# Attention with a bias on one core: q and k of twelve head pairs transposed by DMA instead of by TensorE

## The chip, the core and the metric

The kernel runs on one core of one Trainium2 chip. The metric is device microseconds of one execution; a kernel is given by the median of its runs. The engines are PE (TensorE; PEld is its weight load, which runs beside the matmuls), DVE (VectorE), ACT (ScalarE), POOL (GpSimd) and SP (SyncE, which here only issues DMAs). DMAs issued from SP and ACT go through hardware queues, those issued from POOL through a software queue; all of them run on the core's 16 DMA engines.

## The reference

q, k and v are [4, 8, 1024, 64] in float32, the bias is [1, 1, 1024, 1024] and the same for all 32 heads.

```python
scores = scale * np.matmul(q, k.transpose(0, 1, 3, 2))      # scale = 1/8
scores = scores + bias
scores_max = np.max(scores, axis=-1, keepdims=True)
attn = np.exp(scores - scores_max) / (np.sum(np.exp(scores - scores_max), axis=-1, keepdims=True) + 1e-8)
return np.matmul(attn, v).astype(np.float32)
```

## The kernel before

**Tiling.** The 32 heads are 16 pairs. Rows of the sequence are numbered (p c): partition p holds rows 8p to 8p+7, and chunk c, one of NCH = 8, is the 128 rows with that c. The unit of work is a slot (x, c, h, start): chunk c of the queries of head h, against all 1024 keys, with the scores (keys on the partitions, 8 blocks of 128 queries, 1024 float32 for each partition) in PSUM place x of three. There are 256 slots.

**Scores by difference.** The bias of a chunk is multiplied into a place only where `start` is set (192 matmuls at L220 in all). For the next head in the same place the kernel adds its scores and takes off those of the head before in one matmul of 128 contraction rows: 64 rows hold k and q of the new head, the other 64 hold k and the negated q of the old one. So four arrays [128, 8, 128] stand for each pair:

- `ko`, `qo`: rows 0 to 63 the even head (q negated), rows 64 to 127 the odd head of the same pair. They serve the odd head.
- `ke`, `qe`: rows 0 to 63 the even head of the pair, rows 64 to 127 the odd head of the pair before (q negated). They serve the even head.
- `qs`, `qz`: q of an even head over rows of zeros, for slots with `start`.

**From the inputs to these arrays.** POOL loads k and q of a pair with a cast to bf16 (`load_k` L133, `load_q` L141) into `land` tiles, of which there are three of each kind. DVE lays the two heads side by side (`side_by_side` L148, tiles `kr` and `qr`, two of each). PE transposes 8 blocks of 128x128 into a PSUM bank (`transposes` L177). DVE copies the bank to SBUF (`copy_out`: `ko` L184, `qo` with signs L186), and then fills the second homes of k and q (`double`: `ke` L195, `qe`, `qs` and `qz` L197): rows 0 to 63 of the same pair's `ke`, rows 64 to 127 of the next pair's. Some of the q doubles go to POOL. The ring of arrays has nine places (RING). V goes by two DMAs of 128 KB for each pair (`load_v` L158) straight into `vall`, whose 65th column is 1; only pairs 0 to 3 have V in a landing tile that DVE copies (L472).

**The work of a slot.** PE fills the place with 8 matmuls (`fill_half` L223). ACT takes the exponential of 1024 columns (`exp` L237) into one of nine `E` tiles in bf16; no maximum is taken off. PE multiplies the 8 blocks of E with V and the column of ones (`av` L296) into a PSUM bank of up to seven slots. DVE empties the bank (`evac`: reciprocal of the sums L304, product into `ob` L308, of which there are two; `od` L312 for blocks that DVE exponentiated), and SP stores the result (L313, L321). For 16 slots the exponential runs on DVE, in seven steps (`d_steps` L257 to L280: `dy`, `df`, `dpw`, `dy`, `db`, `db`, `de`).

**The order.** The pairs go in groups of 4, 6 and 6 (GROUPS). Within a group all heads pass once with three chunks (rounds of three slots), then with chunks 3 and 4, then with the three others. So a new pair of the group is first wanted every six slots, and then no new one until the next group. Pairs 4 to 9 are the second group, 10 to 15 the third. `may_d` names the slots that may go to DVE.

The order on every engine is written out by a planner inside the kernel: a loop at the end keeps a clock for PE, ACT and DVE, and at each step lets the engine go on that can start first. It works with fixed costs (an exponential 906 ns, a fill 450, a bank multiplication 265), with due times `ready[...]`, `raw_at`, `land_at`, `v_at` of arrays, layouts and loads, and with priorities for DVE. `pieces` is the list of transpositions that PE still has to make, in the order of the pairs; a piece may go when its pair is at most AHEAD = 60 slots away and a ring place is free. A pair's loads are issued once the q layout three pairs before it is written. What the planner writes is a fixed program; at run time the engines only wait for semaphores.

Of the kernel before, what the change touches and what calls it, by code (L numbers as in the profile page):

```python
# [16 lines left out]
def kernel(  # L17
# [35 lines left out]
    raw = ctx.enter_context(tc.tile_pool(name="raw", bufs=2))  # L53
    kq = ctx.enter_context(tc.tile_pool(name="kq", bufs=RING))
# [19 lines left out]
    b0f = consts.tile([P, S], F32)  # L74
    q0f = consts.tile([P, 2, C0, D], F32)
    q0r = consts.tile([P, 2, NCH - C0, D], BF)
    k0f = consts.tile([P, 2, NCH, D], F32)
# [49 lines left out]
    may_d = [x[0] == 2 and 24 < s < NS - 12 and not any(y[3] for y in slots[s:s + 4]) for s, x in enumerate(slots)]  # L127

    raws, lands, arrs = {}, {}, {}
# [5 lines left out]
    def load_q(pr, cs):  # L135
        if pr == 0:
            lands[0, 0] = q0r
        elif (pr, 0) not in lands:
            lands[pr, 0] = land.tile([P, 2, NCH, D], BF, name="q16")
        to = lands[pr, 0] if pr == 0 else lands[pr, 0][:, :, cs, :]  # L140
        nc.gpsimd.dma_start(out=to.rearrange("p t c d -> p t (c d)"),  # L141
                            in_=qf[pr][:, :, cs.start * D:cs.stop * D])

# [15 lines left out]

    def arrays(pr):  # L160
        if pr not in arrs:
            t = {x: kq.tile([P, NCH, P], BF, name=x) for x in (("ko", "ke", "qo", "qe") if pr else ("ko", "qo"))}
            if pr in split_pair:
                t["qs"] = qs
            if pr in first_pair:
                t["qz"] = qz[group_of[pr] % 2]
            arrs[pr] = t
        return arrs[pr]

    def linked(pr):  # L170
        return pr + 1 < NP
# [28 lines left out]
    def parts(pr, which):  # L200
        return ([0] if pr else []) + ([1] if linked(pr) else []) + (
            [] if which else [2] * (pr in split_pair) + [3] * (pr in first_pair))
# [96 lines left out]
    def evac(b):  # L299
        po, units = bank[b]  # L300
        n = len(units)
        own = [s for s in units if batch_of[s] == b and s not in dslots]
        rs = small.tile([P, 7, 1], F32, name="rs")
        nc.vector.reciprocal(rs[:, :n, :], po[:, :n, D:D1])  # L304
        m = len(own)
        ob = op.tile([P, 6, D], F32, name="ob")
        if m:
            nc.vector.tensor_tensor(ob[:, :m, :], po[:, :m, :D], rs[:, :m, :].to_broadcast([P, m, D]), op=ALU.mult)  # L308
        for j in range(m, n):
            x, c, h, start = slots[units[j]]  # L310
            od = op.tile([P, D], F32, name="od")
            nc.vector.tensor_tensor(od[:], po[:, j, :D], rs[:, j, :].to_broadcast([P, D]), op=ALU.mult)  # L312
            nc.sync.dma_start(out=of[:, h, c, :], in_=od[:])  # L313

        j = 0
        while j < m:
            x, c, h, start = slots[own[j]]
            i = j + 1
            while i < m and slots[own[i]][1:3] == (c + i - j, h):
                i += 1  # L320
            nc.sync.dma_start(out=of[:, h, c:c + i - j, :], in_=ob[:, j:i, :])  # L321
            j = i

    with tc.manual_schedule():
# [66 lines left out]
        EXP = 906  # L391
        T0 = 7400.0
# [14 lines left out]
        q_items += [(p, 0, 0, NCH) for p in range(GROUPS[0], NP)]  # L407
        k_items = [(p, 1, 0, NCH) for p in range(1, NP)]
        n1 = GROUPS[0] - 1
        pieces = [y for x in zip(k_items[:n1], q_items[:n1]) for y in x] + q_items[n1:n1 + GROUPS[0]]  # L410
        pieces += [y for x in zip(k_items[n1:], q_items[n1 + GROUPS[0]:]) for y in x]
# [12 lines left out]
        waiting, free_lands, loads = [], set(), list(range(GROUPS[0], NP))  # L424
        AHEAD = 60
# [16 lines left out]
        def arrange(pr, which, c0, n):  # L442

            if (pr, which, c0) not in land_at:
                waiting.append((pr, which, c0, n))
                return
            urgent = need_at[pr, which, c0] - next_fill < 12
            cost = 60 + 35 * n

            def run(t2):  # L450
                side_by_side(pr, which, slice(c0, c0 + n))
                raw_at[pr, which, c0] = t2 + cost + L_DVE
                if which == 0 and c0 + n == NCH:
                    free_lands.add(pr)
                    while loads and loads[0] - 3 in free_lands:
                        load(loads.pop(0), t2)
            dve_q.append((land_at[pr, which, c0], 0 if urgent else 2, cost, run))

        def load(pr, t):
            load_k(pr)  # L460
            load_q(pr, slice(0, NCH))
            land_at[pr, 1, 0] = dma(pool(t, 750), 1900)
            land_at[pr, 0, 0] = dma(pool(t, 750), 1900)
            load_v(pr)
            v_at[pr] = dma(pool(0, 1900), 5500)
            for x in [x for x in waiting if x[0] == pr]:
                waiting.remove(x)
                arrange(*x)

# [59 lines left out]
        def pe_cands():  # L529
# [59 lines left out]
            if pieces:  # L589
# [4 lines left out]
                if ((pr, which, c0) in raw_at and next_fill >= need - AHEAD and (ring < 0 or last_slot[ring] < next_fill)  # L594
# [6 lines left out]
                    if r < 1e11:  # L601
# [5 lines left out]
                        def end(t, pr=pr, which=which, c0=c0, n=n, tag=tag, cost=cost):  # L607
# [8 lines left out]
                            def run(t2):  # L616
# [3 lines left out]
                                if which:  # L620
                                    ready["ko", pr] = done + L_DVE
                                else:
# [11 lines left out]
        def close(b, tag, t):  # L634
# [4 lines left out]
            def run(t2):  # L639
                evac(b)  # L640
# [67 lines left out]
        while next_fill < NS or next_act < len(acts) or avq or dav or dve_q:  # L708
# [10 lines left out]
            if p:  # L719
                c.append((p[0], 2))  # L720
            if not c:
# [9 lines left out]
            elif who == 1:  # L731
                dve_q.remove(d)
                t_dve = t + d[2]
                d[3](t)
            else:
# [32 lines left out]
```

## Time and profile before

| what | value |
|---|---|
| runs | median 247.41 us of 3 (247.38 to 248.35) |
| profiled execution | 247.3 us, its span 245.5 us (first to last instruction), granted TensorE clock 0.992 |
| ACT, exponentials (L237) | 241 instructions, 223.6 us busy |
| PE, value matmuls (L296), score matmuls (L223) | 89.1 us (1920, with another 6.7 us for DVE's blocks); 76.5 and 62.3 us (1024 and 832, and 192 with `qz` and `qs`) |
| PE, transpositions (L177) | 256 matmuls, 22.5 us busy |
| DVE, 16 exponentials (L257 to L280) | 119.5 us |
| DMA queues | POOL's software queue 36304 packets, 14.06 MB, 50.0% of 16 engines' time; SP's 17664 packets, 9.12 MB, 13.5% |
| stores on SP | 117, median 2.1 us to landing (1.4 to 7.9) |
| loads of k on POOL | 15, 3.7 to 10.3 us to landing, median 5.5 |

How it is read: the busy times of PE overlap, since matmuls are pipelined, so a busy PE is not a PE at its limit. A line stands for all instructions that a source line writes, whatever pair they belong to, so stages are told apart by stretches of the span. The DMA share is the sum of packet times over 16 engines; where several queues are served at once it goes over 1.

### The profile page before, as it was taken

Reading aid. Unit: us, or ns where it says so; the run is one execution under the profiler, and the core shown is the slowest. Engines: PE = TensorE matmul, PEld = TensorE weight load, DVE = VectorE, ACT = ScalarE, POOL = GpSimd, SP = SyncE. Lnnn points to the kernel's source line nnn. Section 1 sums busy time; section 2 is a strip of 40 time slices with the busy share of each in tenths; the row PEclk is TensorE's granted clock in tenths of the full one; section 3 lists DMA queues with packets and bytes.
Section 4 is the critical chain, followed back from the end, with each engine's and each line's share of the span. In section 5 each row is a group of like instructions: output and inputs, shape, how many; then the busy total and the mean of one; then the engine's idle time right before and its main releaser. Section 6 shows DMA issues by size and latency. Waiting matters only on the chain.

```text
span 245.5 us, 10300 instructions
## 1 busy us (share of the span) xinstructions
PE 223.2 (91%) x4554; PEld 211.3 (86%) x4554; DVE 214.5 (87%) x370; ACT 226.7 (92%) x245; POOL 61.9 (25%) x82
## 2 busy tenths in 40 slices
PE   7879999999989898999999988898999999999981
PEld 2779899999989897989999988788999998998871
DVE  3669963989999999999999999999999999499991
ACT  3689999999999989999999998999999999999991
POOL 8837566041313504325000374000000000000000
PEclk9999999999999999999999999999999999999996
DMA  6999999999998697998741391110121021020211
GB/s 211 203 202 171 215 199 198 196 134 110 148 104 109 76 145 127 140 92 133 92 83 31 73 120 29 40 47 19 40 61 42 27 63 28 19 69 27 67 40 37
DMA packets 54155, 24.34 MB, mean 99 GB/s; under 512 B 32352, under 2 KB 53088, under 8 KB 54112
## 3 DMA queue, kind: packets, MB, share of 16 engines
q0 software_dynamic: 36304, 14.06, 50.0%
q1 hardware_dynamic: 17664, 9.12, 13.5%
q8 instruction: 35, 0.57, 1.0%
q10 hardware_dynamic: 144, 0.52, 0.6%
q14 instruction: 8, 0.07, 0.1%
HBM read 29.36 MB, written 8.39 MB: 154 GB/s over the span
## 4 chain that ended last, share of the span: by engine, by line
DVE 41%; PE 29%; ACT 17%; issue 9%; DMA 2%; ACTq 0%; SPq 0%; DVEq 0%
PE pl L223 17%; ACT E L237 17%; PE po L296 7%; DVE qo L186 4%; DVE dy L257 4%; DVE ke L195 4%; DVE ob L308 4%; DVE qe L197 3%; DVE de L280 3%; DVE ko L184 3%; PE pl L220 3%; DVE db L276 3%; DVE dy L269 3%; DVE db L269 2%; DMA k0f<-in_k_dram 2%
## 5 line engine op out<-in xcount | busy, mean ns | idle before, releaser
L237 ACT ACTIVATE E<-pl 128x1024 bf16<-128x1024 f32 (+1 forms) x241 | 223.6, 1072 | 9.1 <-PE pl L223 8.1
L296 PE MATMUL po<-vall,E 128*128 128x65 bf16 x1920 | 89.1, 194 | 6.1 <-DVE ob L308 2.2
L296 PEld LDWEIGHTS <-E 128*128 128x128 bf16 x1920 | 76.5, 98 | 7.9 <-DVE ob L308 3.0
L223 PE MATMUL pl<-qo,ko 128*128 128x128 bf16 x1024 | 76.5, 219 | 3.3 <-ACT E L237 1.6
L223 PEld LDWEIGHTS <-ko 128*128 128x128 bf16 x1216 | 72.4, 98 | 6.6 <-issue 4.6
L223 PE MATMUL pl<-qe,ke 128*128 128x128 bf16 x832 | 62.3, 219 | 4.0 <-DVE qe L197 1.8
L223 PEld LDWEIGHTS <-ke 128*128 128x128 bf16 x832 | 49.7, 98 | 6.2 <-issue 4.5
L308 DVE TENSOR_TENSOR ob<-po,rs 128x384 f32<-128x384 f32 (+3 forms) x44 | 22.9, 521 | 1.8 <-DVE rs L304 0.3
L257 DVE TENSOR_SCALAR dy<-pl 128x1024 int32<-128x1024 f32 x16 | 19.5, 1220 | 4.7 <-ACT E L237 3.5
L133 POOL DMA_DIRECT2D k<-in_k_dram x15 | 11.1, 740 | 46.1 <-DVE kr L148 31.8
L158 POOL DMA_DIRECT2D vall<-in_v_dram x24 | 21.1, 882 | 0.9 <-issue 0.6
L141 POOL DMA_DIRECT2D q<-in_q_dram x18 | 12.9, 719 | 33.2 <-DVE qr L148 26.6
L269 DVE SCALAR_TENSOR_TENSOR dy<-df 128x1024 f32<-128x1024 f32 x16 | 19.5, 1218 | 0.2
L276 DVE SCALAR_TENSOR_TENSOR db<-db,dpw 128x1024 f32<-128x1024 f32 x16 | 19.5, 1219 | 0.2
L280 DVE SCALAR_TENSOR_TENSOR de<-dy,db 128x1024 bf16<-128x1024 f32 x16 | 19.5, 1219 | 0.2
L269 DVE SCALAR_TENSOR_TENSOR db<-df 128x1024 f32<-128x1024 f32 x16 | 19.5, 1219 | 0.0
L220 PE MATMUL pl<-ident,braw 128*128 128x128 bf16 x192 | 16.0, 226 | 0.1
L195 DVE COPY ke<-ko 64x1024 bf16<-64x1024 bf16 x30 | 14.5, 484 | 0.8
L184 DVE COPY ko<-px 128x1024 bf16<-128x1024 bf16 (+1 forms) x17 | 11.1, 651 | 4.2 <-PE px L177 4.2
L186 DVE TENSOR_SCALAR qo<-px,sgn 128x1024 bf16<-128x1024 bf16 (+2 forms) x20 | 12.7, 637 | 2.2 <-PE px L177 2.0
L197 DVE TENSOR_SCALAR qe<-qo 64x1024 bf16<-64x1024 bf16 (+2 forms) x33 | 13.4, 407 | 0.9
L304 DVE RECIPROCAL rs<-po 128x5 f32<-128x5 f32 (+4 forms) x44 | 8.4, 192 | 6.5 <-PE po L296 6.2
(50 smaller groups left out, 153.8 us busy)
## 6 DMA issues: line engine op xcount, KB each, us to landing
out_dram<-ob SPq DMA_DIRECT2D x53, 96.0 KB, 1.9
k<-in_k_dram POOLq DMA_DIRECT2D x15, 256.0 KB, 5.5
q<-in_q_dram POOLq DMA_DIRECT2D x12, 256.0 KB, 5.5
vall<-in_v_dram POOLq DMA_DIRECT2D x24, 128.0 KB, 6.1
out_dram<-ob SPq DMA_DIRECT2D x33, 64.0 KB, 3.3
braw<-in_bias_dram POOLq DMA_DIRECT2D x7, 256.0 KB, 7.3
v<-in_v_dram POOLq DMA_DIRECT2D x4, 256.0 KB, 6.4
b0f<-in_bias_dram ACTq DMA_DIRECT2D x1, 512.0 KB, 4.5
```

The costliest lines, as they stand in the source:

```text
L158: nc.gpsimd.dma_start(out=vall[:, 2 * pr + t, :, :D], in_=vf[pr, :, t])
L186: nc.vector.tensor_scalar(t["qo"][:, cs, :], px[:], sgn[:], None, op0=ALU.mult)
L195: w.tensor_copy(to["ke"][rows, cs, :], t["ko"][rows, cs, :])
L220: nc.tensor.matmul(to, braw[:, c, :].rearrange("p (kp kc) -> p kc kp", kc=NCH)[:, kc, :], ident8[:], start=i == 0, stop=False, skip_group_ ...
L223: nc.tensor.matmul(to, kk[:, kc, :], qq[:, c, :], start=False, stop=True, skip_group_check=True)
L237: nc.scalar.activation(e[:, i:i + n].rearrange("p b x -> p (b x)"), places[slots[s][0]][:, i:i + n].rearrange("p b x -> p (b x)"), ACTF.Ex ...
L257: w.tensor_scalar(y[:], places[slots[s][0]].rearrange("p b x -> p (b x)"), scale * LOG2E * 65536.0, 127.0 * 65536.0, op0=ALU.mult, op1=ALU ...
L269: w.scalar_tensor_tensor(o[:], t["f"][:], c, t["f"][:], op0=ALU.add, op1=ALU.mult)
L276: w.scalar_tensor_tensor(t["b"][:], t["b"][:], V2, t["p"].bitcast(BF), op0=ALU.add, op1=ALU.mult)
L280: w.scalar_tensor_tensor(etile[s].rearrange("p c q -> p (c q)"), t["a"], V1, t["b"][:], op0=ALU.add, op1=ALU.mult)
L296: nc.tensor.matmul(po[:, j, :], etile[s][:, kc, :], vall[:, h, kc, :], start=j == 0 and kc == 0, stop=kc == NCH - 1, skip_group_check=True)
L308: nc.vector.tensor_tensor(ob[:, :m, :], po[:, :m, :D], rs[:, :m, :].to_broadcast([P, m, D]), op=ALU.mult)
```

## The change

For pairs 4 to 15, TensorE's transpositions, the PSUM bank that they pass through, the copies out of it and the doublings of k and q are replaced as follows. Pairs 0 to 3 stay as they were.

- DVE lays out three bf16 tiles for each pair in place of two (`layout_steps`): `kr` as before (one copy of 1024 elements for each partition, L186); `qr` with the even head negated, in two half steps (L190, L195); and `q2`, three buffers, which holds this pair's even head beside the negated odd head of the pair before. Its first half is written with the pair itself (L196), its second with the pair before (`removed`, L150).
- SP issues a DMA transposition of each of them, SBUF to SBUF, straight into the array that PE reads: `kr` to `ko`, `qr` to `qo`, `q2` to `qe` (`turn`, L200), 36 in all, each of 256 KB.
- SP issues plain DMAs for k's second home, rows 0 to 63 of `ke` from the same pair's `ko` (L552) and rows 64 to 127 from the pair before (L541, L555), and for `qs` and `qz` where a pair starts a group or a chunk of slots (L572): 28 in all, each of 64 rows of 2 KB.
- All SP issues, the stores among them, pass through one planned queue (`sp_q`). `evac` hands back its stores, with the `od` ones behind the `ob` ones.
- A pair's V is loaded when the next pair's k and q are (pair 15's with its own).
- The landing buffers of the first bias chunk and of the first k (`b0f`, `k0f`) move into the pool of DVE's exponential (tiles `df` and `db`).
- `may_d` ends 18 slots before the end instead of 12. In the program that comes out, 17 slots have their exponential on DVE, and PE has 64 transposing matmuls.

The diff, cut to its core:

```diff
+    raw2 = ctx.enter_context(tc.tile_pool(name="raw2", bufs=3))
...
-    b0f = consts.tile([P, S], F32)
+    b0f = dp.tile([P, S], F32, name="df")
...
-    k0f = consts.tile([P, 2, NCH, D], F32)
+    k0f = dp.tile([P, S], F32, name="db").rearrange("p (t c d) -> p t c d", t=2, d=D)
...
-    may_d = [x[0] == 2 and 24 < s < NS - 12 and not any(y[3] for y in slots[s:s + 4]) for s, x in enumerate(slots)]
+    may_d = [x[0] == 2 and 24 < s < NS - 18 and not any(y[3] for y in slots[s:s + 4]) for s, x in enumerate(slots)]
...
+    def removed(pr, cs):
+        if pr + 1 not in q2:
+            q2[pr + 1] = raw2.tile([P, NCH, 2, D], BF, name="q2")
+        nc.vector.tensor_scalar(q2[pr + 1][:, cs, 1, :], lands[pr, 0][:, 1, cs, :], -1.0, None, op0=ALU.mult)
...
+    def layout_steps(pr, which):
+        l = lands[pr, which]
+        if which:
+            raws[pr, 1, 0] = t = raw.tile([P, NCH, 2, D], BF, name="kr")
+            return [(340, lambda: nc.vector.tensor_copy(t.rearrange("p c t d -> p t c d"), l[:]))]
+        def first():
+            raws[pr, 0, 0] = t = raw.tile([P, NCH, 2, D], BF, name="qr")
+            nc.vector.tensor_scalar(t[:, :, 0, :], l[:, 0], -1.0, None, op0=ALU.mult)
+        def last():
+            removed(pr, slice(0, NCH))
+        steps = [first, lambda: nc.vector.tensor_copy(raws[pr, 0, 0][:, :, 1, :], l[:, 1]),
+                 lambda: nc.vector.tensor_copy(q2[pr][:, :, 0, :], l[:, 0])]
+        return [(HALF, f) for f in steps + [last] * (pr + 1 < NP)]
+
+    def turn(to, of):
+        nc.sync.dma_start_transpose(to[:], of.rearrange("p c t d -> p c (t d)"))
...
+        ISSUE, TURN, COPY = 70, 4500, 3000
...
-        q_items += [(p, 0, 0, NCH) for p in range(GROUPS[0], NP)]
-        k_items = [(p, 1, 0, NCH) for p in range(1, NP)]
+        k_items = [(p, 1, 0, NCH) for p in range(1, GROUPS[0])]
...
-            load_v(pr)
-            v_at[pr] = dma(pool(0, 1900), 5500)
+            for p in [pr - 1] * (pr > GROUPS[0]) + [pr] * (pr + 1 == NP):
+                load_v(p)
+                v_at[p] = dma(pool(0, 1900), 4800)
...
+        def advance():
+            while turns:
+                pr, which = turns[0]
+                ring = pr + 1 - RING
+                if ((pr, which, 0) not in land_at or next_fill < first_slot[pr] - AHEAD
+                        or ring >= 0 and last_slot[ring] >= next_fill
+                        or pr < GROUPS[0] + 2 and any(y[1] == which for y in pieces)
+                        or pr >= GROUPS[0] + 2 and (pr - 2, which) not in turned
+                        or which == 0 and pr == GROUPS[0] and left_q2
...
+                    return
+                turns.pop(0)
+                prio = 0 if first_slot[pr] - next_fill < 12 else 2
+                steps = layout_steps(pr, which)
...
+                    dve_q.append((max(land_at[pr, which, 0], turned.get((pr - 2, which), 0)), prio, cost, run))
...
+        def turn_k(pr, t):
...
+            turn(a["ko"], raws[pr, 1, 0])
+            done = turned[pr, 1] = ready["ko", pr] = t + TURN
+            def copies(t2):
+                nc.sync.dma_start(out=a["ke"][:D], in_=a["ko"][:D])
+                ready["ke", pr] = t2 + COPY
+                if pr + 1 < NP:
+                    nc.sync.dma_start(out=arrays(pr + 1)["ke"][D:], in_=a["ko"][D:])
...
+            sp_q.append((done, copies))
+
+        def turn_q(pr, t):
...
+            turn(a["qo"], raws[pr, 0, 0])
+            turn(a["qe"], q2[pr])
+            t_sp += ISSUE
+            done = turned[pr, 0] = t + TURN + 1000
...
-                evac(b)
+                for to, of_ in evac(b):
+                    sp_q.append((t2 + cost + L_DVE, lambda t3, to=to, of_=of_: nc.sync.dma_start(out=to, in_=of_)))
```

## The prediction

> **What bounds the kernel now.** I read the page's busy shares first, then its slices, then a table of stages, then who waited for whom in two of them.
>
> The page, parts 1 and 2 (busy us, share of the span, instructions; then tenths in 40 slices of 6.1 us):
> ```profile
> PE 223.2 (91%) x4554; PEld 211.3 (86%) x4554; DVE 214.5 (87%) x370; ACT 226.7 (92%) x245; POOL 61.9 (25%) x82
> ...
> ACT  3689999999999989999999998999999999999991
> ...
> DMA  6999999999998697998741391110121021020211
> ```
> Three engines stand near 90%, so the average decides nothing. ACT runs 240 of the 256 score blocks' exponentials, one after the other, from 9.4 us to 240.1 us, with a head of 9.4 us ahead and a tail of 5.4 us behind.
>
> ACT's table of stages (stretch, its length, busy us, count; then granted clock, DMA share and GB/s):
> ```profile
> 40.00:70.00 30.00, 29.30 (x33) 1.00 1.25 149
> 70.00:100.00 30.00, 28.25 (x31) 1.00 0.93 116
> 100.00:140.00 40.00, 39.84 (x44) 1.00 0.62 90
> 140.00:187.00 47.00, 44.18 (x48) 1.00 0.25 47
> 187.00:240.00 53.00, 52.74 (x58) 1.00 0.16 44
> ```
> Idle ACT is 0.70, 1.75, 0.16, 2.82 and 0.26 us here, plus 1.5 between its first exponential and 40 us: 7.2 us, which is all that a perfect feed could save. In 100 to 140 us and after 187 us ACT is the bound (33 exponentials in 30.69 us of the timeline: 0.930 us each). In 70 to 100 and 140 to 187 us something else is.
>
> The same table for the transposing line L177 (PE busy us and matmuls, then its weight loads):
> ```profile
> 70.00:100.00 30.00, 4.62 (x56) 3.40 (x56) 1.00 0.93 116
> 100.00:140.00 40.00, 1.54 (x16) 1.01 (x16) 1.00 0.62 90
> 140.00:187.00 47.00, 6.77 (x80) 4.99 (x80) 1.00 0.25 47
> ```
> ACT's idle time goes with the transpositions: 56 and 80 where it waits, 16 and none where it doesn't. The waits of 70 to 100 us name the way it goes (us, times, longest):
> ```profile
> PEld L296 <- DVE ob L308: 2.3, 3, 1.1
> ACT E L237 <- PE pl L223: 1.8, 4, 0.7
> PE po L296 <- DVE ob L308: 1.7, 2, 1.0
> ```
> ACT waits for score matmuls (`pl`); those stand on PE behind value matmuls that wait for VectorE to empty a PSUM bank; and VectorE (29.05 of these 30 us busy, 45.76 of the 47) is at copies of transposed q and k or at an exponential of its own.
>
> **The change, part by part.**
>
> PE. The rewritten program holds 64 transposing matmuls instead of 256; 192 go. PE issued 568 matmuls in 26.83 busy us between 70 and 100 us, 47 ns each, so 192 are 9.1 us; at L177's own 6.77/80 = 85 ns they are 16. They are worth only what ACT waits for, so I count them below through ACT.
>
> DVE. Gone are, from the groups by shape:
> ```profile
> L195 DVE COPY ke<-ko 64x1024 bf16<-64x1024 bf16 x30 | 14.5, 484 | 0.8
> ...
> L184 DVE COPY ko<-px 128x1024 bf16<-128x1024 bf16 x15 | 10.2, 682 | 3.5 <-PE px L177 3.5
> L186 DVE TENSOR_SCALAR qo<-px,sgn 128x1024 bf16<-128x1024 bf16 x12 | 8.9, 745 | 0.1
> L197 DVE TENSOR_SCALAR qe<-qo 64x1024 bf16<-64x1024 bf16 x19 | 8.6, 452 | 0.5
> ```
> 24 `ke` x 0.484 = 11.6, 12 `ko` x 0.682 = 8.2, 12 `qo` x 0.745 = 8.9, 19 `qe` x 0.452 = 8.6, three `qs`/`qz` at 0.42 = 1.3 and 12 `qr` x 0.424 = 5.1: 43.7 us. (The 12 `kr` stay in number.) New are 47 half layouts of 128x512, 24 copies and 23 negations, which the trace lacks; their neighbours are `qr` at 250 to 320 ns for 384 and 640 elements and `qe` at 275 and 414 ns. In the middle that is 24 x 0.285 + 23 x 0.345 = 14.8 us, with two smaller pieces 15.5; the ends give 12.3 and 17.9. A 17th VectorE exponential adds its seven rows, 7.5 us. Net -20.7 us: VectorE goes from 214.5 to about 194 us, 79%. POOL loses five doublings (7.1 us), under cover of everything.
>
> ACT. One exponential fewer: 0.93 us.
>
> ACT's waits. I let the two transposing stages idle as 100 to 140 us does, 0.16 in 40 us: 77 us keep 0.3 of their 4.57, so 4.3 us go; of the 0.70 in 40 to 70 us, half. What is late next there is ACT itself. The 1.5 us before 40 us belong to pairs 0 to 3, which are unchanged. Sum 4.6 us.
>
> Tail. At 240.69 us PE multiplies a VectorE block, then comes `od` (0.21 us), and its store goes ahead of the last one (0.38 us). VectorE blocks now end 18 slots before the end instead of 12, and the last bank holds three plain ones: 0.8 us less. If ACT finishes later, this stays.
>
> SP and the DMA engines. New are 36 transpositions of 256 KB and 28 copies of 128 KB, beside the 117 stores. No row shows a transposition. From the queues: SP's queue took 13.5% x 245.5 x 16 / 17664 packets = 30 ns per packet of 516 B, POOL's 54 ns. A transposition split as those stores are is 512 packets, 32 on each engine: 0.95 us; in the 256 B pieces of its source rows it is 64 per engine, 1.9 us at 30 ns, and 3.5 us at POOL's 54 ns, the price of `vall`'s small pieces. Nearest are the 256 B pieces on SP's own queue: I take 1.9, keeping 0.95 and 3.5. Copies at 0.48 us are 13 us in all. On landing: a V half of as many pieces lands in 3.9 to 10.5 us, a store in 1.4 to 7.9.
>
> The Trainium skill bears on this price (DMA: Bandwidth & Descriptors, Latency and other measured facts): it gives DMA transposes 261 GB/s in one kernel, an estimate of 1.0 us for 256 KB. No trace so far shows it. That is about the lower end; by it the DMA engines' load would rise by 36 us instead of 68, and the forecast would keep its 242 with more room.
>
> Whether it is hidden. In the program's order I count the exponentials (0.93 us each) between an array's issue on SP and the first score matmul that reads it. Pair 4: 19 at the least; 5: 21; 6: 19; 7: 15; 8: 11; pair 9's `ke`: 8; pairs 10 to 15: 29 or more. So 7.4 us cover the tightest and 18 us most. V, one pair later, still leads its first use by 35. The new waits on VectorE, for layouts that reuse a buffer read by the transposition two pairs earlier, lie 7 or more exponentials (6.5 us) behind it; behind a layout stand the bank evacuations, and PE waits for those. SP's stores stand behind transpositions that wait for layouts, and VectorE's two `ob` buffers wait for stores. The bias' and first k's landing buffers, now those of the first VectorE exponential, are read at 9 us and reused after 40: nothing. For scattered overruns of these 6.5 us, while loads still fill the queues until 53 us, I put back 0.8 us, one of the gaps that ACT has now.
>
> Sum on the profiled execution: span 245.5 - 4.6 - 0.9 - 0.8 + 0.8 = 240.0; with the 1.8 us that its 247.3 us has around the span, 241.8, and 0.1 more since the median of the runs, 247.41, lies that much above this execution: 241.9, forecast as **242.0 us**.
>
> **Rivals.**
>
> *The arrays of pairs 8 and 9 come late* (slower). From exponential 33 to 80 SP issues 18 transpositions in 47 x 0.93 = 43.7 us, with 7.4 us to spare at the end. If each takes over 51/18 = 2.8 us of SP or of the DMA engines, pair 9 is late. At 3.5 us it is 63 - 51 = 12 us late and ACT stands for it: 254. At 3.1 us the 5.4 us that I expect are used up; beyond that it is slower. For it speaks that the DMA engines are at 0.93 to 1.25 of their time in 40 to 100 us already; against it that 1.62 was reached in 40 to 50 us, and that the competing loads (k, q of pairs 10 to 12, V) have 35 or more exponentials of slack. 22%.
>
> *The waits only change their names.* Layouts on VectorE wait at the head for transpositions, evacuations behind them come as late as now, and the 4.6 us stay: 246.6, or down to 245 if part goes. Idle PE in 70 to 100 us is 3.2 us already, so spare PE time alone feeds nobody. 13%.
>
> *The transposed blocks pass one by one.* If each 128x128 block costs what a lone 32 KB store takes to land, 1.5 us, eight are 12 us: pairs 4 to 9 need 18 x 12 = 216 against 51 us, 165 us late, pairs 10 to 15 216 against 51 x 0.93 + 27 = 74, 142 late: some 550 us. The Trainium skill has such a figure (VectorE: DVE Perf Modes, The three transpose paths): 1309 ns by DMA against 390 ns on TensorE for one 128x128 block. No run here shows it. 3%.
>
> That the change does less than it says is out: the order holds all 36 transpositions, 12 pairs of three.
>
> **How the numbers follow.** Forecast 62%, its own range 239.5 (no overrun, half of the early idle gone too) to 245.5 (1.5 us of waits left, layouts at their upper price). A measurement tells about 0.5% apart, 246.2 to 248.6. Faster: 0.62 and 0.03 of the second rival: 0.65. Same: 0.10 of it and 0.02 of the first: 0.12. Slower: 0.20 and 0.03: 0.23. The range holds the time 8 times in 10 from 239.5 to 250.5, which takes in the first rival up to 3.3 us a transposition.
>
> **What would show it.** Right: L177 at 64 in the groups; VectorE near 194 us; ACT's idle under 0.5 us in 70 to 100 and 140 to 187 us; transpositions that land in under 6.5 us; no wait of PE for a DMA at the score line. Wrong: `pl` waiting for DMA `ke` or `qe` about 75 to 95 us; layouts waiting for `ko` or `qe`; SP's queue held for more than 2.8 us by a transposition; `ob` waiting for stores.

## The result, and the profile after

The changed kernel takes **292.74 us** (median of 4 runs, 290.23 to 296.06) beside 247.39 us for the kernel before on the same chip: 1.179 times as long, 95% interval 1.170 to 1.189. The profiled execution took 296.06 us, its span is 294.3 us. It is the longest of the four (granted clock 0.904, where the others have 0.92 at spans of 288.5 to 291.9 us), so the waits below may be a per cent or so long.

The page after, parts 1 and 2 (the slices are 7.4 us now):
```profile
PE 227.7 (77%) x4362; PEld 215.5 (73%) x4362; DVE 188.0 (64%) x343; ACT 226.6 (77%) x244; POOL 55.1 (19%) x77
...
ACT  3789998640049995659998189876489999999994
...
DMA  7999999999998999955999579989601111112111
```
The work fell as the change meant it to: PE has 192 matmuls fewer, VectorE 26.5 us less to do, ACT is as busy as before. But ACT's row now has holes in slices 8 to 30, where the DMA engines stand mostly at 9; once their row falls to 1, ACT is at 9 to the end.

ACT's table of stages (stretch, length, busy us, count; granted clock, DMA share, GB/s):
```profile
70.00:100.00 30.00, 14.35 (x16) 0.70 1.28 155
...
140.00:187.00 47.00, 37.88 (x41) 0.89 1.32 141
```
Before, 70 to 100 us had 28.25 us busy at a DMA share of 0.93. The second row holds other work than the same time held before: between 40 and 140 us ACT now does 69 exponentials, where it did 108. It is about the work of 100 to 140 us before, which had 39.84 of 40 us busy at a share of 0.62.

Who waited for whom, first a row of before, then after (us, times, longest):
```profile
ACT E L237 <- PE pl L223: 8.1, 15, 2.0
...
ACT E L266 <- PE pl L252: 57.7, 32, 21.3
...
DVE ob L339 <- DMA out_dram<-ob: 35.8, 8, 15.7
PE pl L252 <- DVE dy L286: 29.6, 6, 21.6
...
DVE q L150 <- DMA qe<-q: 7.8, 2, 5.8
DVE qr L190 <- DMA qo<-qr: 7.6, 3, 4.2
```
ACT's row is the effect: 57.7 us instead of 8.1. The cause is to be sought in the rows in which VectorE waits for a DMA: 35.8 + 7.8 + 7.6 = 51.2 us, where the span grew by 48.8 us; that the two sums are so near is partly chance, since not every wait of VectorE holds up ACT. PE's wait for `dy` is a wait for VectorE, which had to take a PSUM place and stood. The chain that ended last says the same, by engine, before and after:
```profile
DVE 41%; PE 29%; ACT 17%; issue 9%; DMA 2%; ACTq 0%; SPq 0%; DVEq 0%
PE 30%; DMA 23%; ACT 16%; DVE 12%; issue 12%; SPq 6%; ACTq 0%; DVEq 0%
```

How one such wait comes about: first VectorE's evacuation whose stores are waited for, then the chain of waits around the longest wait (start us, us, what):
```profile
47.53 0.49 DVE L339 TENSOR_TENSOR ob<-po,rs 128x320 f32<-128x320 f32 x1
...
65.26 3.83 SPq L200
...
69.18 1.72 SPq L749
...
71.45 8.79 DMA out_dram<-ob
...
80.36 0.49 DVE ob L339
...
83.40 1.01 PE pl L252 x8
```
Read downwards: a bank is emptied by 48.0 us. Its three stores are issued from 69.18 us on, the last at 71.45, when SP is through with a transposition that held it 3.83 us and with what stood ahead of that. The last store takes 8.79 us to land. Until then VectorE can't write `ob` for the next bank but one and stands for 15.7 us. Behind that evacuation wait VectorE's own exponential and, with it, PE. So of the 32 us from the emptied bank to the landed store, 23 pass in SP's queue. SP's timeline in the same place shows it without a pause:
```profile
48.13 4.99 SPq L200 DMA_TRANSPOSE qe<-q  x1
53.22 5.17 SPq L200 DMA_TRANSPOSE ko<-kr  x1
...
59.79 5.37 SPq L200 DMA_TRANSPOSE qo<-qr  x1
65.26 3.83 SPq L200 DMA_TRANSPOSE qe<-q  x1
```
The time that SP spends on one issue, before it can turn to the next, is called a hold here. The 36 transpositions hold SP 95.1 us in all, 2.64 us each, and land 3.1 to 16.1 us after their issue, median 8.0.

My theory after this: the transpositions and the loads need more of the DMA engines than there is before about 190 us; everything on SP gets late, stores too, and VectorE, which works in order, hands that to PE and ACT. Rivals: the transposition itself is dear; SP's queue, not the engines, is short; two `ob` buffers are the whole cause; PE's and VectorE's new order is.

### The profile page after: what moved, and what is told of

Its sections match the earlier page's. It is cut to its first block, busy times and chain, and to the rows that moved or that the text cites. A ratio compares the mean times of both kernels' runs of the same rounds, so it can differ in the third digit from the quotient of the medians.

```text
span 294.3 us, 10034 instructions
## 1 busy us (share of the span) xinstructions
PE 227.7 (77%) x4362; PEld 215.5 (73%) x4362; DVE 188.0 (64%) x343; ACT 226.6 (77%) x244; POOL 55.1 (19%) x77
## 3 DMA queue, kind: packets, MB, share of 16 engines
q0 software_dynamic: 36304, 14.06, 44.5%
## 4 chain that ended last, share of the span: by engine, by line
PE 30%; DMA 23%; ACT 16%; DVE 12%; issue 12%; SPq 6%; ACTq 0%; DVEq 0%
PE pl L252 18%; ACT E L266 16%; DMA out_dram<-ob 11%; PE po L325 9%; DMA qe<-q 5%; DMA ke<-ko 3%; SPq L200 2%; SPq L749 2%; DVE dy L286 2%; DVE de L309 2%; PE pl L249 2%; DMA qo<-qr 2%; DMA db<-in_k_dram 2%; DVE ob L339 1%; PE px L206 1%
## 5 line engine op out<-in xcount | busy, mean ns | idle before, releaser
L266 ACT ACTIVATE E<-pl 128x1024 bf16<-128x1024 f32 (+1 forms) x240 | 223.4, 1095 | 58.8 <-PE pl L252 57.7
L252 PE MATMUL pl<-qo,ko 128*128 128x128 bf16 x1024 | 83.2, 229 | 32.6 <-DVE dy L286 29.4
L252 PEld LDWEIGHTS <-ko 128*128 128x128 bf16 x1216 | 78.2, 102 | 36.9 <-issue 34.2
L325 PE MATMUL po<-vall,E 128*128 128x65 bf16 x1912 | 94.8, 198 | 4.0 <-DVE od L352 1.9
L325 PEld LDWEIGHTS <-E 128*128 128x128 bf16 x1912 | 81.9, 101 | 4.8 <-DVE od L352 2.0
L252 PE MATMUL pl<-qe,ke 128*128 128x128 bf16 x832 | 67.2, 228 | 15.9 <-DMA ke<-ko 6.9
L252 PEld LDWEIGHTS <-ke 128*128 128x128 bf16 x832 | 54.3, 103 | 19.5 <-issue 13.5
L339 DVE TENSOR_TENSOR ob<-po,rs 128x384 f32<-128x384 f32 (+3 forms) x44 | 22.9, 520 | 37.1 <-DMA out_dram<-ob 35.8
L286 DVE TENSOR_SCALAR dy<-pl 128x1024 int32<-128x1024 f32 x17 | 20.7, 1220 | 11.4 <-PE pl L252 6.2
L135 POOL DMA_DIRECT2D k<-in_k_dram x15 | 10.7, 710 | 86.5 <-DVE kr L186 86.5
L334 DVE RECIPROCAL rs<-po 128x6 f32<-128x6 f32 (+4 forms) x44 | 8.5, 193 | 25.2 <-PE po L325 25.0
L166 POOL DMA_DIRECT2D vall<-in_v_dram x24 | 21.7, 909 | 2.5 <-DMA vall<-in_v_dram 1.2
L298 DVE SCALAR_TENSOR_TENSOR db<-df 128x1024 f32<-128x1024 f32 x17 | 20.7, 1218 | 0.0
L143 POOL DMA_DIRECT2D q<-in_q_dram x18 | 13.0, 722 | 25.7 <-issue 10.7
L249 PEld LDWEIGHTS <-braw 128*128 128x128 bf16 x192 | 13.9, 148 | 0.8 <-issue 0.8
L325 PE MATMUL po<-vall,de 128*128 128x65 bf16 x136 | 7.4, 198 | 7.1 <-DVE de L309 7.1
L291 DVE TENSOR_SCALAR df<-dy 128x1024 f32<-128x1024 uint16 x17 | 11.7, 686 | 0.1
L295 DVE TENSOR_SCALAR dpw<-dy 128x1024 int16<-128x1024 int16 x17 | 11.6, 685 | 0.0
```

Of the source, the lines that this page charges most:

```text
L166: nc.gpsimd.dma_start(out=vall[:, 2 * pr + t, :, :D], in_=vf[pr, :, t])
L249: nc.tensor.matmul(to, braw[:, c, :].rearrange("p (kp kc) -> p kc kp", kc=NCH)[:, kc, :], ident8[:], start=i == 0, stop=False, skip_group_ ...
L252: nc.tensor.matmul(to, kk[:, kc, :], qq[:, c, :], start=False, stop=True, skip_group_check=True)
L266: nc.scalar.activation(e[:, i:i + n].rearrange("p b x -> p (b x)"), places[slots[s][0]][:, i:i + n].rearrange("p b x -> p (b x)"), ACTF.Ex ...
L286: w.tensor_scalar(y[:], places[slots[s][0]].rearrange("p b x -> p (b x)"), scale * LOG2E * 65536.0, 127.0 * 65536.0, op0=ALU.mult, op1=ALU ...
L291: w.tensor_scalar(t["f"][:], t["lo"], G / 65536.0, None, op0=ALU.mult)
```

## The experiments

Unless it says otherwise, an edit is made to the changed kernel. The kernel before took 246.9 to 247.1 us beside each set. In runs 3, 4, 5, 8, 9, 10, 13 and 14 the traces show the same instructions in the same order on PE, VectorE and ACT as in the changed kernel; in runs 2, 6, 7, 11, 12 and 15 to 18 the planner wrote another order, so these differ by more than their edit.

**1. The price by itself.** No attention is computed: phases of transpositions, V pieces, rows of k and copies, alone and together.
```diff
+    a = phase([], turns("ta", 6, kr))
+    a = phase(a, pieces("pb", 6))
+    a = phase(a, turns("tc", 6, kr), pieces("pc", 6))
```


> No attention in it: it measures prices alone. Six DMA transpositions of 256 KB back to back; then six V halves (1024 packets of small pieces each); then six of both at once; then four k loads in long rows; four transpositions with four such loads; six copies of 64 rows; three transpositions with one store behind them. Theory 'packets' (the DMA engines have too many small packets, and a transposition and V's pieces take turns): a transposition alone takes about 2.5 us (64 packets for each engine at the 38 ns that SP's queue shows), beside V's pieces 5 to 6 us, beside long rows about 3 to 4 us. Theory 'order' (SP's in-order queue is the cause and the price of a transposition is fixed): about 5 us each, alone or not. Under both the store behind three transpositions lands only after them, 7 us or more.

SP's holds, alone and beside six V pieces (min/median/max ns, first and last start):
```profile
L41 SPq DMA_TRANSPOSE ta<-kr x6: 1309/1329/1357, 3.8 to 10.7; - x6
L41 SPq DMA_TRANSPOSE tc<-kr x6: 1232/2124/3457, 24.3 to 36.0; - x6
```
Alone, six start 1.38 us apart (6.9 us for five steps) and land in 3.2 to 3.4 us; beside V pieces they land in 3.1 to 9.7, and the pieces in 7.6 instead of 4.4 (medians). From the first issue to the last landing, six of each took 10.1 and 9.2 us alone and 16.5 together: little of it overlaps. Both expected prices were too high for a lone transposition; it is dear only in company. A store behind three transpositions was issued 4.1 us after the first of them and landed 2.3 us later, a little sooner than expected: with idle engines its delay is the queue's. An estimate from these phases: a pair's three transpositions are 4.1 us of the engines, its two V pieces 3.1, its k and q in rows (8.8 us for four) 4.4, so 11.6 us and the copies and stores on top, while the second group asks for a new pair every six exponentials, 5.6 us. It is too high, since the phases contain landings: without the transpositions it gives 7.5, and the kernel before lived with that.

**2. V in rows.** V of pairs 4 to 15 lands in rows of 2 KB and VectorE copies it into place, as it did for pairs 0 to 3.
```diff
-        if pr < GROUPS[0]:
+        if True:
             lands[pr, "v"] = vland.tile([P, 2, NCH, D], BF, name="v16")
...
```


> The changed kernel with V of pairs 4 to 15 loaded in long rows into the landing tile and moved by VectorE (12 copies of about 0.43 us), as pairs 0 to 3 are: some 21500 small packets less on POOL's queue, about 70 us of the DMA engines' time. Theory 'packets': the waits for stores and layouts shrink to a few us, 243 to 256 us. Theory 'order': SP's queue holds the same transpositions ahead of the same stores, so at least 280 us.

287.33 us (282.11 to 288.69). POOL's packets fell from 36304 to 14608, SP's mean hold from 2.64 to 2.22 us and the waits for `ob` only to 25.9 us. So fewer packets of V alone don't do it here. How much they cost stays open: VectorE's copies wait 6.7 us for V, and the order is another.

**3. Stores on POOL.**
```diff
-  ... nc.sync.dma_start(out=to, in_=of_)
+  ... nc.gpsimd.dma_start(out=to, in_=of_)
```


> The changed kernel with its stores issued from POOL instead of SP, all else in place. Theory 'order': the 35.8 us in which VectorE waits for stores go, and with them 30 us or more: 250 to 262 us. Theory 'packets': stores land earlier, but layouts wait for transpositions and loads stay as slow: 272 to 290 us.

308.01 us, ratio 1.235 (1.232 to 1.237); waits for `ob` 57.5 us. POOL's loads now stand behind stores that wait for VectorE, and stores behind loads. It made a second in-order queue late, and couldn't tell queue from engines.

**4. Three `ob` buffers.**
```diff
-    op = ctx.enter_context(tc.tile_pool(name="op", bufs=2))
+    op = ctx.enter_context(tc.tile_pool(name="op", bufs=3))
```


> The changed kernel with three ob and od buffers instead of two: an evacuation waits for a store that is one batch (some 5.5 us) older. Theory 'order': the 8 waits for stores get up to 5.5 us shorter each, 262 to 280 us. Theory 'packets': the wait comes back at the next instruction, 280 to 293 us.

283.0 us, 1.134 (1.127 to 1.142), within the second theory's range. The wait for `ob` fell from 35.8 to 13.2 us, and PE's for `ke` rose from 6.9 to 11.4.

**5. Plain copies in place of the transpositions.** Same issues, same bytes, nothing transposed, so the scores are those of other data.
```diff
-        nc.sync.dma_start_transpose(to[:], of.rearrange("p c t d -> p c (t d)"))
+        nc.sync.dma_start(out=to[:], in_=of.rearrange("p c t d -> p c (t d)"))
```


> The changed kernel with each transposition written as a plain DMA of the same 256 KB between the same tiles on SP: the transposing itself is left out, so the scores are wrong, but all dependencies, queues and buffers stay. Theory 'price' (the transposing DMA itself holds SP 2.6 us in the mean and fills the engines' rings with 1024 small pieces): a plain copy holds SP some 0.5 us and lands in 2 to 4 us, and the time falls to 239 to 247 us. Theory 'plan' (the new order, its layouts and its two ob buffers stall whatever the DMA costs): above 265 us.

252.26 us, 1.022 (1.019 to 1.025), between the two expectations. With the program's order as it is, 40 of the 45 us go: the order isn't the cause. The copies hold SP 0.74 us each instead of 2.64, but they land hardly sooner, in 7.1 us (median) instead of 8.0. So it is less the late landing than the hold on SP that costs the time. But 5 us stay, so even cheap transfers in the transpositions' place didn't give the forecast.

**6. Pairs 10 to 15 alone by DMA**; pairs 4 to 9 by TensorE as before.
```diff
+    TF = GROUPS[0] + GROUPS[1]
...
-        turns = [(p, x) for p in loads for x in (1, 0)]
+        turns = [(p, x) for p in loads if p >= TF for x in (1, 0)]
...
```


> Only pairs 10 to 15 go by DMA, 18 transpositions; pairs 4 to 9 go through TensorE as before. Theory 'price': the stretch up to 90 us, where loads fill the DMA engines, is then as before, and what is lost is the stores that stand behind three transpositions later on (2.6 us each with loads beside them): 248 to 262 us. Theory 'packets in all' (the sum of small pieces is what counts): half of the loss stays, 265 to 272 us.

**7. k alone by DMA**, 12 transpositions; q by TensorE.
```diff
-        turns = [(p, x) for p in loads for x in (1, 0)]
+        turns = [(p, 1) for p in loads]
...
```


> Only k goes by DMA, 12 transpositions one at a time; q goes through TensorE and VectorE as before. Theory 'price': SP holds 12 x 2 us, never three in a row, and stores are late by 2 to 3 us at most, which two ob buffers bear: 243 to 253 us. Theory 'packets in all': a third of the loss, 260 to 265 us.

258.7 us, 1.048 (1.044 to 1.052), and 258.89, 1.048 (1.046 to 1.050). Half and a third of the transpositions, 9.0 and 8.8 us of waits for `ob`. Both lose about 12 us, far less than all 36, and neither gains.

**8. Five `ob` buffers** (room made by sharing three small tiles).
```diff
-    op = ctx.enter_context(tc.tile_pool(name="op", bufs=2))
+    op = ctx.enter_context(tc.tile_pool(name="op", bufs=5))
...
```


> The changed kernel with five ob and od buffers (the first q landing tile, the zeros and the first q layout moved into buffers of VectorE's exponential). With five, an evacuation waits for a store some 27 us old. Theory 'price': the waits for stores (35.8 us with two, 13.2 with three) go to under 3 us, the waits of layouts and of PE for transposed arrays stay or grow: 262 to 280 us. If the stores were the whole cause it would be under 255.

285.39 us, 1.151 (1.143 to 1.158). Who waited:
```profile
PE pl L252 <- DMA ke<-ko: 14.4, 4, 6.0
...
DVE q L150 <- DMA qe<-q: 13.5, 4, 4.1
```
No store holds VectorE any more, and the time is only 7 us shorter, above what either theory allowed: the same lateness now shows at the layouts' buffers (`q`, with 12.5 us `qr` and with 10.7 us `kr`) and at `ke`. The `ob` buffers were where it showed first, not the cause.

**9. V loads of pairs 4 to 15 left out** (their products read the V of pairs 0 to 3).
```diff
-        for t in range(2):
-            nc.gpsimd.dma_start(out=vall[:, 2 * pr + t, :, :D], in_=vf[pr, :, t])
+        return
...
```


> The changed kernel without the 24 loads of V of pairs 4 to 15; value matmuls of those pairs read V of pairs 0 to 3, so that part of the output is wrong. It takes the small pieces of POOL's queue out of the transpositions' way and adds nothing elsewhere. Theory 'competition' (a transposition is dear only beside other packets: 1.33 us alone, 2.1 to 2.3 beside loads in the price run): the mean hold of SP falls from 2.6 to under 1.7 us and the time to 250 to 265 us. Theory 'transposition alone' (even undisturbed ones are too slow for this order): above 272 us.

260.22 us, 1.053 (1.048 to 1.057): 32 of the 45 us go with 3 MB of loads. SP's mean hold is 1.91 us (under 1.7 was expected), transpositions land in 5.5 us instead of 8.0, and VectorE still waits 16.3 us for `ob`.

**10. Plain copies and five `ob` buffers** (runs 5 and 8 together; scores as in 5).

> Plain copies in place of the transpositions, and five ob buffers: the change as if a transposition cost a plain copy and no evacuation waited for a store. It tests the gain that was forecast apart from the new waits. Theory 'waits at the head of VectorE' (the 252 us of plain copies are 8.1 us of waits for stores and 3.3 us for layouts): 240 to 245 us. If the change's gain was wrong as well: 247 us or more.

249.29 us, 1.008 (1.005 to 1.011). By its expectation the gain that was forecast isn't there either. After 40 us VectorE waits 4.7 us for DMAs, 2.8 of them for `qo`. ACT still stands 13.8 us for PE, and PE 6.5 us for `ke`; ACT's two longest gaps, 3.8 and 3.2 us, lie between 82 and 95 us, where the copies of `ke` land in 6 to 7 us. Beside run 8, which differs from it by the transposing alone, it is 36 us shorter, though both sets of 36 transfers land in the same time (median 7.4 and 7.2 us): they hold SP 0.64 us each here and 2.54 there.

**11. The planner told the truth** (five `ob` buffers too): 9 us for a transposition's landing and 6 for a copy's.
```diff
-        ISSUE, TURN, COPY = 70, 4500, 3000
+        ISSUE, TURN, COPY = 70, 9000, 6000
```


> The changed kernel with five ob buffers, and with the planner told that a transposition lands after 9 us (4.5 before) and a copy after 6 (3 before), as the trace has it. Theory 'waits at the head of VectorE': layouts that would wait are written later, VectorE's waits for DMAs fall from 37 us (five ob) to under 12 us, what is left is PE's waits for late arrays of pairs 7 to 9: 255 to 270 us. Theory 'SP and the engines cannot keep up in the second group whatever the order': above 275 us.

281.88 us, 1.135 (1.124 to 1.145), as the second theory had it. PE waits 21.7 us for `ke`. A plan that reckons with the landings as traced doesn't hide them.

**12. Runs 6, 8 and 11 together**: pairs 10 to 15 alone, five `ob` buffers, the planner told.

> Only pairs 10 to 15 by DMA, five ob buffers, landing told as 9 and 6 us. The third group's arrays have 29 or more exponentials of slack. Theory 'waits at the head of VectorE': the 9.0 us for stores and 6.1 us for layouts of the third-group run go, ACT's idle in 140 to 187 us shrinks by 1 to 2 us against the kernel before: 245 to 249 us. Otherwise 253 us or more.

249.34 us, 1.007 (1.003 to 1.010). No store holds VectorE, and its layouts wait 2.7 us for transpositions. ACT has gaps in the third group's stretch, 1.75 us at 128 and 2.50 at 157 us.

**13. Stores on ACT's queue**, with two `ob` buffers.
```diff
-  ... nc.sync.dma_start(out=to, in_=of_)
+  ... nc.scalar.dma_start(out=to, in_=of_)
```


> The changed kernel with one word altered: the stores of ob are issued on ScalarE's queue instead of SP's, so that they no longer stand behind the transpositions, and not behind POOL's loads either; they still share the 16 DMA engines with both. Before is 247.4 us, the changed kernel 292.7. Theory 'SP's queue in its order' (the stores are late because SP is held 2.6 us by each transposition ahead of them): a store lands within 5 us of its issue, VectorE's wait for ob falls from 35.8 to under 12 us, and the time comes to 265 to 278, since the layouts' and arrays' waits stay as with more ob buffers. Theory 'the engines' (the stores are late because the 16 engines are full of transpositions and loads, whatever the queue): landings of stores stay above 8 us in 40 to 100 us, ob's wait stays at 25 us or more and the time at 285 to 296. ScalarE pays its issues: 117 at an estimated 0.05 to 0.4 us, taken from SP's row, and it can stand for a late ob itself.

317.91 us, 1.284 (1.278 to 1.289): worse than either expectation, since ACT, in order too, now stands at its head for `ob` and, through it, for everything (20.7 us laid to `ke`, 13.4 to `qo`). The question was the landing. `ob` stores between 40 and 100 us, from SP in the kernel before, from SP in the changed kernel and from ACT in this run:
```profile
DMA to landing us min/median/max: 1.6/3.7/6.4
...
DMA to landing us min/median/max: 1.6/7.7/10.1
...
DMA to landing us min/median/max: 3.4/7.3/10.5
```
With no transposition ahead of them in their queue the stores land as late, counted from their issue. The Trainium skill (DMA: Bandwidth & Descriptors, Issuing engines are not separate DMA queues) says that DMAs run on the same 16 engines and interleave whichever engine started them; the landing times of the last two rows agree. But a landing is counted from the issue, so these rows can't clear SP's queue: the time that a store stands behind transpositions lies ahead of it. The traces have both parts, when each store is put to the evacuation that it stores. For banks emptied between 40 and 100 us, all with two `ob` buffers (means in us):

| run | from the emptied bank to the store's issue (longest) | from issue to landing | SP held, of these 60 us |
|---|---|---|---|
| before | 0.5 (2.4) | 3.6 | 13.5 |
| changed | 8.4 (25.3) | 6.7 | 50.2 |
| 5, plain copies | 2.3 (9.3) | 6.0 | 31.5 |
| 9, no V loads | 5.7 (12.7) | 3.4 | 53.6 |
| 13, stores on ACT | 2.0 (9.5) | 7.5 | 50.1 |

Both theories hold a part. The engines make landings 3 us longer, and that goes with V's loads (run 9). SP's queue adds 8 us ahead of the issue, and more than half of it stays when landings are as before. SP is held 50 of 60 us, 34.8 of them by 12 transpositions. Run 5, late in landing and short in the queue, loses 5 us; run 9, the other way round, 13.

**14. No V loads and five `ob` buffers** (runs 8 and 9 together, V as in 9).

> Leaves out the V loads of pairs 4 to 15 (their value products read the V of pairs 0 to 3) and has five ob buffers, otherwise the changed kernel, with all 36 transpositions. The two together take away the loads that compete for the DMA engines and the wait that the stores cause. Without the V loads it was 260.2 us with 16.3 us of waits for ob; with five ob buffers alone 285.4, the waits going to the layouts. Theory 'two causes that add' (transpositions beside loads are slow, and two ob buffers hand that to VectorE): the ob waits go and are not replaced, 243 to 250 us. Theory 'transpositions alone are too many for SP in the second group': the waits move to q, qr, kr and ke as they did with five ob buffers, over 10 us of them, and the time stays at 254 to 262.

256.99 us, 1.031 (1.024 to 1.039); the profiled execution has a span of 251.6 us. PE's waits for a DMA at the score line, and the stretch of ACT after them:
```profile
87.45 1.03 PE L251 MATMUL pl<-qe,ke 128*128 128x128 bf16 x8 [4.90 <-DMA ke<-ko]
...
104.39 1.01 PE L251 MATMUL pl<-qe,ke 128*128 128x128 bf16 x8 [4.87 <-DMA ke<-ko]
```
```profile
107.64 43.38 ACT L265 ACTIVATE E<-pl 128x1024 bf16<-128x1024 f32 x47 [0.21 <-PE pl L251]
```
The second theory's signs came: no wait for `ob` on VectorE is left, but layouts wait 9.3 us and PE 11.5 us for `ke`, and the time lies in its range. What stays is the second group's arrays, late at PE's head in the stretch for which the first rival was written. It is SP's queue: 18 transpositions hold it 35.4 us between 40 and 100 us, stores and copies another 18.7, while stores land in 3.4 us (mean) as before. The copy of `ke` that ends the last of these waits is issued at 102.05 us, though its `ko` landed at 98.52: two transpositions and stores stand ahead of it. In the third group ACT goes on without a gap past the end of this view, to 164.8 us (62 exponentials).

**15 to 17. Run 12 with V out of the third group's way**: in rows (15, as in run 2), issued ahead of its pair by a growing lead (16), and both (17). The edit of 16:
```diff
-            for p in [pr - 1] * (pr > GROUPS[0]) + [pr] * (pr + 1 == NP):
+            while vq and vq[0] <= pr + max(0, pr - GROUPS[0]) // 2:
+                p = vq.pop(0)
...
```


> The run with pairs 10 to 15 alone transposed by DMA, five ob buffers and a planner told 9 and 6 us (249.34 us before now, span 246.5, ScalarE idle 2.57 us in 70 to 100, 3.25 in 100 to 140 and 3.0 in 140 to 190), with V of pairs 4 to 15 landing in rows of 1024 elements and copied into place by VectorE: 21696 packets of POOL's queue fewer, 12 copies on VectorE more (an estimated 0.4 to 0.7 us each, from the kr row). Before is 247.0. Theory 'what is left is the DMA engines shared with the loads': the gaps of 100 to 190 us go (6.2 us), 243 to 246, faster than both kernels. Theory 'what is left is VectorE's and PE's order, not the DMAs': 248 to 252, the copies add to it.

> The same kernel (pairs 10 to 15 alone by DMA, five ob buffers, planner told 9 and 6 us), with V of pairs 4 to 15 issued on POOL ahead of its pair by a growing lead (pairs 4 and 5 with their own loads, V of 15 with the loads of pair 12), so that no V piece is under way in most of the third group's transpositions. No work is added or removed. Theory 'what is left is the DMA engines shared with the loads': the DMA share in 100 to 140 us falls from 1.20 to about 0.9, the gaps at 128 and 157 us go, 243 to 246.5 us, unless the V pieces disturb 40 to 100 us instead. Theory 'VectorE's and PE's order': 248 to 251, gaps where they were.

> Both of the two edits before: V in rows with a copy on VectorE, and issued ahead. Theory 'the DMA engines shared with the loads': the lowest of the three, 242 to 245 us. Theory 'VectorE's and PE's order': 248 to 252.

257.04 us, 1.037 (1.031 to 1.043), for the rows: above both theories; the copies wait for V (5.9 us) at VectorE's head. **244.26 us**, 0.990 (0.988 to 0.991), for V ahead: faster than both kernels, by 1% than the one before. 246.26, 0.995 (0.992 to 0.998), for both edits, between the two theories. Between runs 12 and 16 the edit of V's order is the only one, and 16 is 5.1 us shorter. But the planner reckons with V, and from VectorE's 75th instruction on the orders of VectorE and PE differ too, so how much of the 5.1 us is the room that V left isn't shown. In 16 the 18 transpositions hold SP 1.66 us each and land in 4.0 us (median); no layout or array waits for one. ACT's last piece:
```profile
101.15 99.66 ACT L267 ACTIVATE E<-pl 128x1024 bf16<-128x1024 f32 x108 [5.12 <-PE pl L253]
```
108 exponentials without a gap (the view ends at 200 us, the row at 238 with 149), through the stretch in which the kernel before idles 2.82 us. The 5.12 us ahead of it, while TensorE still transposes the second group, were not followed up.

**18. The kernel before with the two other edits of run 16** (five `ob` buffers, V ahead), nothing transposed by DMA.

> The kernel before, with no transposition by DMA at all, but with the two other edits of the run that was faster (five ob buffers; V of pairs 4 to 15 issued ahead by the same growing lead). Before is 247.0 us, the run with pairs 10 to 15 transposed by DMA and these two edits 244.26. Theory 'the transpositions by DMA of the third group gain, once the loads are out of their way': this one stays at 246 to 248. Theory 'the gain is that of V ahead or of the buffers, and the transpositions give nothing': 243.5 to 245.

258.48 us, 1.047 (1.045 to 1.048), above both theories. The edits alone don't give run 16's gain. But the planner's order came out differently, with one gap of 9.84 us for ACT at 98 us in which VectorE was busy and no DMA late; so this is no measure of what the transpositions by themselves save.

## Why the prediction was wrong, by its steps

- **PE and VectorE: right.** 4362 matmuls. The 47 half layouts took 14.2 us (24 copies at 0.285, 23 negations at 0.32) against 14.8. VectorE came to 188.0 us against 194; `kr`'s copies (0.42 instead of 0.53 us) are 1.3 of the rest, which I didn't trace further.
- **The price of a transposition: inside its bounds, and of no help.** I took 1.9 us, and alone it is 1.38. 256 KB at that pace are 190 GB/s, below the 261 that the Trainium skill gives (DMA: Bandwidth & Descriptors, Latency and other measured facts). The bounds were for one at a time on engines with room; beside the loads each held SP 2.64 us. What failed is the room: I took from 1.62 in one stretch that a DMA share of 0.93 to 1.25 leaves some. After, a share of 1.28 to 1.58 went with 138 to 155 GB/s, hardly more than the 116 to 149 before. Run 1 shows the same: transpositions and V pieces overlap by 2.8 of 19.3 us.
- **Whether it is hidden: the step that failed.** The sentence was "for scattered overruns of these 6.5 us ... I put back 0.8 us". These waits of VectorE for DMAs measure 51.2 us. I counted cover from SP's issue to PE's use, as if the issue were on time and landings were those of before, and I never added up SP's own time. It was held 50.2 of the 60 us between 40 and 100 us, and stores waited 8.4 us (mean) for their issue there instead of 0.5; they landed in 7.7 us instead of 3.7 (medians), transpositions in 8.0. Each late one was met first by an in-order VectorE at a buffer, far ahead of PE's use. I had named that chain (stores behind transpositions, two `ob` buffers) and given it no price.
- **ACT's waits, -4.6 us: borne out in part, for the third group.** In runs 14 and 16 that transposing stage runs with almost no gap once loads are out of the way, though 16 has an order of its own. For the second group no run gained; plain copies (run 10) still left PE to wait for `ke`.
- **First rival: the right resource, another place, too small.** It was to decide at 2.8 us of SP or engines each for 18 transpositions. The 18 that began between 30 and 130 us held SP 50.2 us, 2.79 each, so by its sum the time would be 242 or little more. It left out SP's other issues, and it counted waits of PE for arrays (`ke`, 6.9 us) and not those of VectorE. Only where neither `ob` nor V's loads stand in the way (run 14) is it the rival as written, at a lower threshold: an estimate from that run's 18.7 us of stores and copies is (51 - 18.7)/18 = 1.8 us, and its transpositions took 2.0.
- **Second and third rival.** The second had a mechanism that came, layouts that wait at VectorE's head for transpositions (15.4 us), but the waits grew instead of changing names. The third is refuted: eight blocks of 128x128 pass in 1.38 us, not 12.
- **The signs.** All that were listed as wrong came, one of them elsewhere: layouts waiting for `qe` (and for `qo`), SP held over 2.8 us, `ob` waiting for stores, and `pl` waiting for `ke`, but at 115 and 125 us.

Settled: the transposing DMAs cost the time and not the program's order (runs 5 and 10); they do it mainly by holding SP's in-order queue, longer beside the loads than alone (runs 1 and 9 and the table of run 13); and the place where it shows moves with the buffers (4, 8). Open: what makes a hold longer beside loads, what of the 5 us of run 5 belongs to which wait, and how much of run 16's gain is the transpositions'.

## What to carry to other kernels

Before work is moved to DMA, add up two times for each stage, by prices measured together with the loads: what the DMA engines need, and how long the issuing queue is held, stores included. In this kernel a DMA share near 1 was no sign of spare room. Then follow each late landing to the first in-order engine that meets it, mostly at a buffer that it wants back, not at the data's reader. Where a stage is full, try to move transfers out of it first: the same 18 transpositions lost 2 us in run 12 and gained 3 in run 16, with V's loads earlier and the order that the planner made of it.

## What the runs showed of the hardware

- A DMA transposition of 256 KB held its issuing queue 1.33 us with idle engines (run 1), and 2.64 us in the mean and up to 5.6 in the changed kernel. A plain copy of the same size held it 0.74 us beside the same loads (run 5).
- A high DMA share is not a rate of bytes: 1.28 to 1.58 went with 138 to 155 GB/s in the changed kernel, and 0.98 with 366 GB/s in run 1's last 22 us, plain stores of 256 KB one after the other.
- The granted clock went with idle PE: 0.70 in 70 to 100 us of the changed kernel, where PE is busy 16.2 of 30 us, and 1.00 before. Eight score matmuls behind the wait of 21.6 us took 1.01 us, where eight took 0.61 at full clock before, so the stall cost a second time.
